# Sixteen rows apart instead of side by side: another assignment of DRAM blocks to SBUF partitions in a top-2 dispatch kernel

## The chip, the cores and the metric

The kernel runs on one core of a Trainium2 chip. The metric is device time in microseconds (us): 239.35 us is the median of three runs of the kernel before (239.24 to 239.37). One further execution was taken with the hardware profiler; all durations of single instructions and transfers come from that one.

## The reference

Each of 16 x 1024 tokens has a row of 512 floats (`x`) and 8 router logits. The softmax over the logits is taken, the two largest probabilities are kept and divided by their sum, and the row is written twice, once multiplied by the smaller and once by the larger of the two:

```
probs = softmax(router_logits)                     # over 8 experts
topk_indices = np.argsort(probs, axis=-1)[..., -k:]    # k = 2
topk_probs = np.take_along_axis(probs, topk_indices, axis=-1)
topk_probs = topk_probs / np.sum(topk_probs, axis=-1, keepdims=True)
return x[:, :, None, :].repeat(k, axis=2) * topk_probs[..., None]
```

So 33.55 MB of `x` and 0.52 MB of logits are read, and 67.11 MB are written. The arithmetic is one multiplication for each float written.

## The kernel before

**Tiling.** The 16384 tokens are 128 partitions times M = 128 rows. They are cut into two groups, `GROUPS = [69, 59]`: group 0 is the first 128 x 69 tokens, group 1 the other 128 x 59. Within a group each partition has one block of consecutive tokens (69 or 59 rows of 2 KB). The views `x_v`, `o_v` and `rl_v` (lines 93 to 95) say which block: partition p has block p. For a load of n rows each partition gets one run of n x 2 KB from DRAM; a store of n rows takes one run of n x 4 KB from each partition. Neighbouring partitions lie 69 x 2 KB = 138 KB (118 KB in group 1) apart in `x` and twice that in the output.

**Loads.** `LOADS` lists them: 7, 32 and 30 rows in group 0, and 30 and 29 rows in group 1 (line 114). After the first load come the two loads of the logits (lines 107 and 108). All are issued from SyncE (SP). The tile `xs` has 69 rows a partition, so the loads of group 1 overwrite rows of group 0, and wait until these have been used and stored.

**Weights.** `top2_weights` (lines 43 to 70) finds the two largest logits by maxima and minima on VectorE (DVE) and makes both weights `WA` with two sigmoids on ScalarE (ACT).

**Products and stores.** `STORES` lists five stores in group 0 and four in group 1, each of 13 to 15 rows. For each, VectorE multiplies rows of `xs` by their two weights in one instruction (line 128); in some of the pieces ScalarE does the last 1 or 4 rows (line 136). The products go to a second tile `osp` or to rows of `xs` that are already used up, by turns, and are stored from there (line 139), again from SP. An instruction that writes `osp` waits until the store that read it before has landed.

**Order.** Nothing is planned: the order of the program is the order on each engine. SP issues loads and stores in that order, one queue for all, and a store's issue waits for its product. All 16 transfers go through this one queue, `q1` in the profile, and each is spread over the core's 16 DMA engines.

## Time and profile before

| | us |
|---|---|
| median of three runs | 239.35 |
| the profiled execution, its own time | 241.59 |
| its span, first to last instruction | 239.8 |
| VectorE busy | 127.9 |
| ScalarE busy | 18.2 |
| DMA queue, share of 16 engines' span | 97.9% |

The profiled execution took 2.24 us longer than the median run, and 1.79 us of it lie outside its span. The line `DMA` of the page gives the mean busy share of the 16 DMA engines in 40 slices of 6 us, the line `GB/s` what they moved; a transfer's piece (packet) is booked in the slice in which it begins, so that a share of a short stretch can be above 1 and neighbouring slices swing around their mean. "SPq" is the issuing of transfers by SyncE.

### The profile page before, as it was taken

How to read it: one execution, taken by the hardware profiler on the slowest of the kernel's cores; microseconds unless marked ns; L12 is line 12 of the kernel's file. 1: busy time of each engine (PE TensorE's matmuls, PEld its weight loads, DVE VectorE, ACT ScalarE, POOL GpSimd, SP SyncE). 2: the span in 40 equal slices, each digit the busy share in tenths (PEclk: the TensorE clock that was granted, in tenths of full speed). 3: DMA queues.
4: the chain of work that ended last, by engine and by line, in shares of the span. 5: the costliest groups of instructions: out<-in, count | busy, mean ns of one | idle time of the engine just before them, and what ended most of it. 6: DMA issues, size and time to landing. Idle time of an engine off the chain costs nothing.

```text
span 239.8 us, 132 instructions
## 1 busy us (share of the span) xinstructions
DVE 127.9 (53%) x20; ACT 18.2 (8%) x29; POOL 0.2 (0%) x4
## 2 busy tenths in 40 slices
DVE  0410299997499990780000000999993999950000
ACT  2000000000440000700000000200000800000000
POOL 0000000000000000000000000000000000000000
DMA  7998989979999989999999799797979979979993
GB/s 263 480 503 372 482 348 492 451 344 440 459 459 459 440 373 411 459 459 448 426 426 460 328 492 471 327 476 332 482 338 492 482 338 492 482 338 481 450 450 172
DMA packets 2304, 101.19 MB, mean 422 GB/s; under 512 B 256, under 2 KB 384, under 8 KB 512
## 3 DMA queue, kind: packets, MB, share of 16 engines
q1 hardware_dynamic: 2304, 101.19, 97.9%
HBM read 34.08 MB, written 67.11 MB: 422 GB/s over the span
## 4 chain that ended last, share of the span: by engine, by line
DMA 53%; DVE 35%; SPq 1%; issue 0%; DVEq 0%
DMA xs<-in_x_dram 26%; DVE osp L128 22%; DMA out_dram<-osp 17%; DVE xs L128 13%; DMA out_dram<-xs 10%; SPq L108 0%; SPq L107 0%; SPq L114 0%; DVEq L128 0%; SPq L139 0%
## 5 line engine op out<-in xcount | busy, mean ns | idle before, releaser
L128 DVE TENSOR_TENSOR osp<-xs,WA 128x14336 f32<-128x14336 f32 (+3 forms) x5 | 62.7, 12532 | 75.7 <-DMA xs<-in_x_dram 58.9
L128 DVE TENSOR_TENSOR xs<-xs,WA 128x14336 f32<-128x14336 f32 (+1 forms) x4 | 61.4, 15359 | 0.3
L136 ACT ACTIVATE osp<-xs,WA 128x512 f32<-128x512 f32 x26 | 16.4, 709 | 161.2 <-DMA out_dram<-osp 113.2
L55 DVE TENSOR_TENSOR osp<-osp 128x512 f32<-128x512 f32 x1 | 0.7, 691 | 9.1 <-DMA osp<-in_router_logits_dram 9.1
L69 ACT ACT_TABLE_LOAD x1 | 1.3, 1283 | 0.7 <-PEq L157 0.7
L69 ACT ACTIVATE WA<-osp 128x128 f32<-128x128 f32 x1 | 0.3, 316 | 11.0 <-DVE osp L68 11.0
L56 DVE TENSOR_TENSOR osp<-osp 128x512 f32<-128x512 f32 x1 | 0.7, 693 | 0.0
L65 DVE TENSOR_TENSOR osp<-osp 128x256 f32<-128x256 f32 (+1 forms) x2 | 0.7, 353 | 0.0
L63 DVE TENSOR_TENSOR osp<-osp 128x256 f32<-128x256 f32 (+1 forms) x2 | 0.7, 352 | 0.0
L64 DVE TENSOR_TENSOR osp<-osp 128x256 f32<-128x256 f32 (+1 forms) x2 | 0.7, 352 | 0.0
L62 DVE TENSOR_TENSOR osp<-osp 128x256 f32<-128x256 f32 (+1 forms) x2 | 0.7, 352 | 0.0
L68 DVE TENSOR_TENSOR osp<-osp 128x128 f32<-128x128 f32 x1 | 0.3, 291 | 0.0
L70 ACT ACTIVATE WA<-osp 128x128 f32<-128x128 f32 x1 | 0.3, 296 | 0.0
L157 POOL MEMSET const-bfloat16-1.0<- 128x1 bf16 x1 | 0.1, 101 | 0.0
L157 POOL MEMSET const-uint8-127<- 128x1 uint8 x1 | 0.1, 101 | 0.0
L157 POOL MEMSET const-float32-0.0<- 128x1 f32 x1 | 0.1, 98 | 0.2 <-issue 0.2
L157 POOL MEMSET const-float32-1.0<- 128x1 f32 x1 | 0.1, 98 | 0.0
## 6 DMA issues: line engine op xcount, KB each, us to landing
out_dram<-xs SPq DMA_DIRECT2D x3, 7168.0 KB, 24.6
xs<-in_x_dram SPq DMA_DIRECT2D x2, 7680.0 KB, 40.0
out_dram<-osp SPq DMA_DIRECT2D x2, 7680.0 KB, 22.3
out_dram<-osp SPq DMA_DIRECT2D x2, 7168.0 KB, 21.3
out_dram<-xs SPq DMA_DIRECT2D x1, 7680.0 KB, 22.3
xs<-in_x_dram SPq DMA_DIRECT2D x1, 7424.0 KB, 53.3
out_dram<-osp SPq DMA_DIRECT2D x1, 6656.0 KB, 23.2
xs<-in_x_dram SPq DMA_DIRECT2D x1, 1792.0 KB, 6.9
```

The lines of the kernel that those rows point to most:

```text
L55: nc.vector.tensor_tensor(hi, a, b, op=ALU.max)
L56: nc.vector.tensor_tensor(lo, a, b, op=ALU.min)
L62: nc.vector.tensor_tensor(tmp, lo[:, :, 0:n], lo[:, :, n : 2 * n], op=ALU.max)
L63: nc.vector.tensor_tensor(nlo, a, b, op=ALU.min)
L64: nc.vector.tensor_tensor(nlo, nlo, tmp, op=ALU.max)
L65: nc.vector.tensor_tensor(nhi, a, b, op=ALU.max)
L68: nc.vector.tensor_tensor(dlt, hi, lo, op=ALU.subtract)
L69: nc.scalar.activation(WA[:, :, 0], dlt[:, :, 0], ACTF.Sigmoid, scale=-1.0)
L70: nc.scalar.activation(WA[:, :, 1], dlt[:, :, 0], ACTF.Sigmoid, scale=1.0)
L128: nc.vector.tensor_tensor(og[:, :v], xs[:, s : s + v, :].unsqueeze(2).to_broadcast([P, v, 2, D]), w[:, :v].unsqueeze(3).to_broadcast([P, v ...
L136: nc.scalar.activation(og[:, i, c], xs[:, s + i, :], ACTF.Copy, scale=w[:, i, c : c + 1])
L157: nc = _bacc.Bacc("TRN2", target_bir_lowering=False, num_devices=1)
```

## The change

Only the three views are changed. They cut the first dimension of a group into 8 x 16 blocks, `(b a m)`, and name `a` before `b`. The partitions of the tiles, 128 in one dimension, are met in the order a, then b: partition 8a + b gets the block of rows 16b + a of its group, where before it got block 8a + b. Logits, `x` and output are changed alike, so each token's weights are still in the partition of its row. The sizes of the runs, the number of loads and stores, their order, every instruction of VectorE and ScalarE and the tiles are as before. The view of DRAM now has dimensions 16, 8 and the rows in place of 128 and the rows, and its first two steps are those of one block (16 of them) and of 16 blocks (8 of them).

```diff
-        x_v.append(xf[t0:t1].rearrange("(p m) d -> p m d", p=P))
-        o_v.append(of[t0:t1].rearrange("(p m) k d -> p m k d", p=P))
-        rl_v.append(rf[t0:t1].rearrange("(p m) e -> p m e", p=P))
+        x_v.append(xf[t0:t1].rearrange("(b a m) d -> a b m d", a=16, b=8))
+        o_v.append(of[t0:t1].rearrange("(b a m) k d -> a b m k d", a=16, b=8))
+        rl_v.append(rf[t0:t1].rearrange("(b a m) e -> a b m e", a=16, b=8))
...
-            nc.sync.dma_start(xs[:, s : s + n, :], x_v[g][:, r : r + n, :])
+            nc.sync.dma_start(xs[:, s : s + n, :], x_v[g][:, :, r : r + n, :])
...
-            {"SP": nc.sync, "ACT": nc.scalar}[queue].dma_start(o_v[g][:, r : r + n], og)
+            {"SP": nc.sync, "ACT": nc.scalar}[queue].dma_start(o_v[g][:, :, r : r + n], og)
```

## Prediction

> **What bounds the kernel now.** I read the page's shares and slices first, then the DMA part, then the chain of waits in order of time, and last short windows of the DMA engines.

> ```profile
> span 239.8 us, 132 instructions
> DVE 127.9 (53%) x20; ACT 18.2 (8%) x29; POOL 0.2 (0%) x4
> ...
> GB/s 263 480 503 372 482 348 492 451 344 440 459 459 459 440 373 411 459 459 448 426 426 460 328 492 471 327 476 332 482 338 492 482 338 492 482 338 481 450 450 172
> DMA packets 2304, 101.19 MB, mean 422 GB/s; under 512 B 256, under 2 KB 384, under 8 KB 512
> ...
> q1 hardware_dynamic: 2304, 101.19, 97.9%
> ```

> The 16 DMA engines carry a packet 97.9% of the span, 0.979 x 239.8 = 234.8 us on each; 5.0 us are left. VectorE works 53% and has slack. The packets number 2304: 16 transfers x 128 partitions is 2048, and the 256 under 512 B are 16 for each transfer. So each partition's run is one packet.

> ```profile
> out_dram<-xs SPq DMA_DIRECT2D x3, 7168.0 KB, 24.6
> out_dram<-osp SPq DMA_DIRECT2D x2, 7680.0 KB, 22.3
> xs<-in_x_dram SPq DMA_DIRECT2D x1, 1792.0 KB, 6.9
> ```

> A store of 7168 KB is 57344 B a partition, and each DMA engine takes 8 such packets.

> ```profile
> 46.00:63.00 17.00, 12.68 (x1) 0.00 (x0) 0.00 (x0) 1.00 1.00 435
> 130.00:148.00 18.00, 0.00 (x0) 0.00 (x0) 0.00 (x0) 1.00 1.01 435
> ```

> These windows (columns: stretch, length, busy time of DVE, ACT and POOL, clock, DMA share, GB/s) show a stretch of stores and one of loads. Both run at 435 GB/s with the engines full, 27.2 GB/s each: reading DRAM and writing it cost alike. At that rate 101.19 MB take 232.6 us. The kernel is bound by 16 streams that each already run at one common rate; the most that any better order could save is 239.8 - 232.6 = 7.2 us, part of which is the start and the last landing.

> ```profile
> 46.60:47.60 1.00, 1.00 (x1) 0.00 (x0) 0.00 (x0) 1.00 0.26 115
> 47.60:48.00 0.40, 0.40 (x1) 0.00 (x0) 0.00 (x0) 1.00 3.97 1720
> 48.00:48.20 0.20, 0.20 (x1) 0.00 (x0) 0.00 (x0) 1.00 1.32 573
> 48.20:48.40 0.20, 0.20 (x1) 0.00 (x0) 0.00 (x0) 1.00 0.00 0
> ```

> A packet is booked where it begins. 115 GB/s over 1 us are 2 packets of 57344 B, 1720 over 0.4 us are 12, 573 over 0.2 us are 2: all 16 engines begin a packet within 0.6 us at most. They march in step, with 57344 B / 27.2 GB/s = 2.11 us a packet.

> ```profile
> 89.48 24.60 DMA out_dram<-xs
> ...
> 114.09 36.16 DMA xs<-in_x_dram
> ...
> 150.38 15.10 DVE osp L128
> ...
> 165.50 0.02 SPq L139
> ```

> ```profile
> 162.00:162.80 0.80, 0.80 (x1) 0.00 (x0) 0.00 (x0) 1.00 2.23 965
> 162.80:164.90 2.10, 2.10 (x1) 0.00 (x0) 0.00 (x0) 1.00 0.20 85
> 164.90:166.30 1.40, 1.31 (x2) 0.00 (x0) 0.00 (x0) 1.00 0.10 42
> 166.30:166.60 0.30, 0.30 (x1) 0.00 (x0) 0.00 (x0) 1.00 7.21 3072
> 166.60:167.60 1.00, 1.00 (x1) 0.00 (x0) 0.00 (x0) 1.00 0.14 61
> ```

> At one place in the chain the queue runs dry. The second group's first load lands at 150.25 us, VectorE takes 15.10 us, and the store is issued at 165.5 us, when most engines have done the last load. Of its packets (59392 B, 2.18 us each) 13 begin from 162.0 to 162.8 and end by 165.0; the next to begin, 15 at once (3072 GB/s over 0.3 us, of 61440 B), are the store's at 166.3. The sixteenth engine begins its own over 0.3 us later (61 GB/s, one packet). I put this hole at 1.4 us, 164.9 to 166.3.

> **The change part by part.** *Work.* The bytes, the run lengths and the 16 issues stay, and the work of VectorE and ScalarE is untouched. The line rate gives the same 232.6 us if the 16 engines still work at 27.2 GB/s each.

> *Issue.* The DRAM side now has one dimension more.

> ```profile
> L114 SPq DMA_DIRECT2D xs<-in_x_dram x5: 339/531/1219, 0.7 to 114.5; - x5
> L139 SPq DMA_DIRECT2D out_dram<-osp x5: 332/332/348, 43.6 to 198.0; - x5
> ```

> An issue takes 0.33 to 0.34 us at its fastest (columns after the colon: min/median/max ns). The trace has no issue of this shape. From below it costs nothing more, or even less; from above I double it, 0.34 us each. It lies beside running transfers except at the first load and at the dry place, so the upper end is 2 x 0.34 = 0.7 us, and 16 x 0.34 = 5.4 us if every issue counted. I take 0, as the number of descriptors is unchanged. The work hiding it is the queue's stock: the store at 89.48 us landed 24.60 us after issue, some 17 us of which are its own bytes (7.34 MB / 435 GB/s), so 7 us of older work lay ahead of it. Nothing is queued on SP behind an issue but the next wait for a product.

> *DRAM addresses.* Before, neighbouring partitions were 138 KB apart in `x`; now one step of b is 16 blocks, 2208 KB. Reads and writes, at different strides (138 KB in `x`, 276 KB in the output), ran alike at 435 GB/s, so I take 0 for this; from both sides, a gain is at most the 7.2 us above, and a loss is bounded by the slowest long slice of the page, 327 GB/s, 1.33 times as long.

> *Which engine serves which partition.* This is the term that decides. Before, both sides of a transfer counted 128 in one dimension, so the 128 packets could be dealt to the 16 engines in any pattern. Now the DRAM side counts 16, then 8, and the SBUF side 128. Both can be cut alike for 16 engines only as 16 consecutive pieces: engine a has partitions 8a to 8a + 7, in this order. My hypothesis for this kernel: the ways into SBUF are sixteen, each good for the 27.2 GB/s that one stream has in the windows, and each serving certain groups of partitions; before, each engine kept to one way, and now two engines are on the same way at a time, while half the ways are idle. The trace before shows no such sharing. Bounds from its rows: at the one end the packets still take 2.11 us (no effect; below that they can't go, since all 16 are at their rate); at the other, two streams at one rate, 4.2 us a packet, twice the 234.8 us.

> [...]

> *How far in step.* Let the two engines of a pair be apart by a lead. A run on one way is 4 packets, 8.4 us. During the lead they aren't in each other's way, so time is (2 - lead/run) times the present. All begin within 0.6 us, which is at most 7% of a run; but the late engine of the windows from 162.8 to 167.6 us shows that one can get behind by some packet's part: it begins one load packet in the hole, after the other engines' last ones began by more than 2 us (24%). Equal sharing keeps a lead as it is. I take 5%: a factor of 1.95.

> The sum: 234.8 x 1.95 = 457.9, plus the 5.0, minus the 1.4 us hole (the 29 rows that cover it now take twice as long, against unchanged 15.10 us of VectorE): a span of 461.5. With the 1.79 us outside the span, 463.3 stands against the profiled execution's 241.59. The median of the runs is 2.24 us lower: 461. No new wait opens: VectorE's 127.9 us are far below, and stores land later but queue behind as many older bytes as now, so that the queue stays full.

> **The rivals.** *Pairs that drift apart.* If one engine of a pair gets more of the shared way, it pulls ahead until it is on the other way while its partner is on the first; from then on both run at full rate. For it: 0.6 us is no firm lock, and a lead of 2 us occurs. Against: nothing in the rows favours one engine steadily. A single full run's lead costs 8.4 us, 239.35 + 8.4 = 248; half way, a factor of 1.4 gives 239.35 + 0.4 x 234.8 = 333. So 250 to 414 for part, ending where it becomes my forecast (1.75).

> *Nothing happens.* If each engine's rate is its own limit and not SBUF's, or the pieces are dealt as before, the 2.11 us a packet stay and the time is 239.35. The windows speak for it in so far as an engine's rate and a way's rate can't be told apart there.

> *Slightly slower.* DRAM addresses or the longer issue take some per cent: 5.4 us of issues give 244.8. Against: all covers named above. 240 to 250.

> *Faster, by one mechanism.* The late engine holds back the first load of the second group, and with it the store at 165.5 us. If its lateness comes from its DRAM blocks, and the new blocks end it while the engines keep 27.2 GB/s, the load lands earlier and the hole of 1.4 us closes: 237.9. It decides as soon as that load lands 1.4 us before 150.25. Against: no other window shows an engine that late, so it looks like a single event.

> **How the numbers follow.** The forecast, pairs sharing, has 0.54; its own range goes from a factor of 1.75 (234.8 x 1.75 + 5.0 - 1.4 - 0.45 = 414; 0.45 is 2.24 - 1.79) to a factor of 2 with the hole kept and all issues dearer (469.6 + 5.0 - 0.45 + 5.4 = 480). Partial drift has 0.20, slightly slower 0.08, nothing 0.13, faster 0.05. A measurement of this kernel tells about 0.2%, 0.5 us, from no change. Slower is 0.54 + 0.20 + 0.08 = 0.82, same 0.13, faster 0.05. Leaving out same and faster (0.18) and a little of the rest, the range is 243 to 480.

> **What would show it.** Right: the slices' GB/s fall to about 220 over the whole span, the DMA share stays above 95% (each engine still holds a packet all the time), a 7168 KB store lands some 45 us after its issue in place of 24.6, the hole before the first store of group 1 is gone, and VectorE's 127.9 us stay. Packets stay at 2304; more of them would mean that runs were cut. A share near 50% at the same 220 GB/s would mean that only 8 engines are used: the time of the forecast by another cause. Full rate with one pair-like lag between early and late engines would show drift. Unchanged 435 GB/s in the windows would show the hypothesis wrong at its root: engines, not ways into SBUF, set the rate.

## The result and the profile after

The changed kernel takes 443.51 us (median of four runs, 437.46 to 444.64) against 239.36. The ratio is 1.839, with a 95% interval of 1.820 to 1.859; it is taken from the two faster of the four runs (437.46 and 442.92), as the other two count as slow, and the medians as they stand give 1.853. Its profiled execution is the fastest of the four, 437.46 us with a span of 435.7.

The page of the changed kernel, the lines that answer to those shown of before:

```profile
span 435.7 us, 132 instructions
## 1 busy us (share of the span) xinstructions
DVE 127.9 (29%) x20; ACT 18.2 (4%) x29; POOL 0.2 (0%) x4
...
GB/s 179 243 253 217 187 181 254 197 300 205 247 211 253 247 200 253 279 258 205 282 274 266 214 231 217 218 218 249 332 265 299 271 197 237 259 244 238 253 137 21
DMA packets 2304, 101.19 MB, mean 232 GB/s; under 512 B 256, under 2 KB 384, under 8 KB 512
## 3 DMA queue, kind: packets, MB, share of 16 engines
q1 hardware_dynamic: 2304, 101.19, 95.6%
```

The same bytes move in the same 2304 packets, VectorE is as busy as before, and the DMA engines still hold a packet 95.6% of the span. They only move 232 GB/s instead of 422. Each packet takes longer; nothing else is added. The last two slices (137 and 21 GB/s) are new: the engines no longer finish together.

Windows of the changed kernel: one stretch of the first group's loads, the first group's stores, the second group's loads, the second group's stores.

```profile
54.00:86.00 32.00, 30.12 (x2) 0.00 (x0) 0.00 (x0) 1.00 1.02 211
90.00:242.00 152.00, 35.68 (x3) 10.02 (x16) 0.00 (x0) 1.00 1.01 251
244.00:312.00 68.00, 31.25 (x2) 1.33 (x2) 0.00 (x0) 1.00 0.99 233
316.00:433.00 117.00, 26.98 (x2) 5.01 (x8) 0.00 (x0) 1.00 0.87 226
```

The first group's loads run at 211 GB/s where 435 stood before, a factor of 2.06. Stores are a little better: 251 GB/s over the first group (the last 12 us of that window hold loads of the second group too), and 226 over the second, where the share of 0.87 says that some engines were already without work. The second group's loads, which follow the stores, run at 233.

The DMA issues and the issuing lines of the changed kernel:

```profile
out_dram<-xs SPq DMA_DIRECT2D x3, 7168.0 KB, 69.0
out_dram<-osp SPq DMA_DIRECT2D x2, 7680.0 KB, 50.1
...
xs<-in_x_dram SPq DMA_DIRECT2D x1, 1792.0 KB, 10.9
```

```profile
L115 SPq DMA_DIRECT2D xs<-in_x_dram x5: 586/598/2552, 0.7 to 215.9; - x5
L140 SPq DMA_DIRECT2D out_dram<-osp x5: 537/538/591, 69.1 to 356.2; - x5
```

The stores of these rows land 50 to 69 us after their issue in place of 22 to 25, and an issue takes 0.54 to 0.59 us at its fastest in place of 0.33 to 0.34. The latter is real, but 16 times 0.25 us beside running transfers explains nothing of 200 us.

### The profile page after: what moved, and what is told of

Read it like the earlier page. It is cut to its first block, busy times and chain, and to the rows that moved or that the text cites. A ratio compares the mean times of both kernels' runs of the same rounds, so it can differ in the third digit from the quotient of the medians.

```text
span 435.7 us, 132 instructions
## 1 busy us (share of the span) xinstructions
DVE 127.9 (29%) x20; ACT 18.2 (4%) x29; POOL 0.2 (0%) x4
## 2 busy tenths in 40 slices
DMA packets 2304, 101.19 MB, mean 232 GB/s; under 512 B 256, under 2 KB 384, under 8 KB 512
## 3 DMA queue, kind: packets, MB, share of 16 engines
q1 hardware_dynamic: 2304, 101.19, 95.6%
## 4 chain that ended last, share of the span: by engine, by line
another core or an unknown queue 34%; DVE 26%; DMA 25%; SPq 0%; issue 0%; DVEq 0%
DMA out_dram<-osp 22%; DVE osp L129 14%; DVE xs L129 10%; DMA osp<-in_router_logits_dram 3%; DVE osp L55 0%; DVE osp L56 0%; SPq L115 0%; SPq L108 0%; DVE osp L64 0%; DVE osp L65 0%; DVE osp L63 0%; DVE osp L62 0%; DVE osp L68 0%; DVEq L129 0%
## 5 line engine op out<-in xcount | busy, mean ns | idle before, releaser
L69 ACT ACTIVATE WA<-osp 128x128 f32<-128x128 f32 x1 | 0.3, 315 | 15.6 <-DVE osp L68 15.6
## 6 DMA issues: line engine op xcount, KB each, us to landing
out_dram<-xs SPq DMA_DIRECT2D x3, 7168.0 KB, 69.0
xs<-in_x_dram SPq DMA_DIRECT2D x2, 7680.0 KB, 76.4
out_dram<-osp SPq DMA_DIRECT2D x2, 7680.0 KB, 50.1
out_dram<-osp SPq DMA_DIRECT2D x2, 7168.0 KB, 52.4
out_dram<-xs SPq DMA_DIRECT2D x1, 7680.0 KB, 65.0
xs<-in_x_dram SPq DMA_DIRECT2D x1, 1792.0 KB, 10.9
```

Source lines behind the costliest of these rows:

```text
L69: nc.scalar.activation(WA[:, :, 0], dlt[:, :, 0], ACTF.Sigmoid, scale=-1.0)
```

## The experiments

### The same mixing, cut 32 x 4 and 64 x 2

```diff
-        x_v.append(xf[t0:t1].rearrange("(b a m) d -> a b m d", a=16, b=8))
+        x_v.append(xf[t0:t1].rearrange("(b a m) d -> a b m d", a=32, b=4))
...
```

`o_v` and `rl_v` are changed alike; the second kernel has a=64, b=2.

> The views keep the mixing of the blocks but cut 32 x 4 in place of 16 x 8: partition 4a + b gets block 32b + a. The DRAM side counts 32, then 4, so each engine can be given two groups of four neighbouring partitions that need not be side by side. Theory of the ways into SBUF (the cut decides which partitions an engine has at a time): each engine can keep to one way, packets of 57344 B take 2.11 us, 239.4 us within 1%. Rival, DRAM addresses (neighbouring blocks read and written by all engines at once, and large steps within a partition group): as with 16 x 8, about 440 us. Rival, a third dimension on the DRAM side makes transfers slow by itself: about 440 us too. [...]

> The views cut 64 x 2: partition 2a + b gets block 64b + a. As with 32 x 4 each engine can be given groups of four neighbouring partitions. Theory of the ways: 239.4 to 242 us. The 32 x 4 cut took 0.9% over the kernel before. If that is the price of a third dimension in each issue (0.67 us in place of 0.38 for the first), it is the same here, 241.6; if it is the order of the blocks in DRAM, it may differ, 239.4 to 241.6. Rival, mixing of blocks as such: about 440.

Measured: 241.65 us for 32 x 4 (1.0089 of before, 1.0068 to 1.0110) and 241.64 us for 64 x 2 (1.0071, 1.0040 to 1.0102). Windows of the 32 x 4 kernel, a stretch of stores and one of loads, and its issuing of loads:

```profile
47.00:63.00 16.00, 12.02 (x1) 0.00 (x0) 0.00 (x0) 1.00 0.99 430
134.00:148.00 14.00, 0.00 (x0) 0.00 (x0) 0.00 (x0) 1.00 1.00 430
```

```profile
L115 SPq DMA_DIRECT2D xs<-in_x_dram x5: 591/612/1389, 0.7 to 115.1; - x5
```

The blocks are mixed here too, neighbouring blocks are in use at once, and the DRAM view has three dimensions with the dearer issue. All of that together costs 2.2 to 2.3 us. Both rivals fall. What the 16 x 8 cut does beyond it costs 202 us. Where the 2.3 us come from isn't settled: the two mixings cost the same, which fits the issue, but the first issue explains only 0.3 us (0.67 us with 32 x 4 against 0.38 before), and single runs of the kernel before take 241.3 us too; its profiled execution took 241.59.

### The cut alone, blocks side by side

```diff
-GROUPS = [69, 59]
+GROUPS = [69, 58]
...
-        t1 = t0 + P * n
-        x_v.append(xf[t0:t1].rearrange("(b a m) d -> a b m d", a=16, b=8))
...
+        t1 = t0 + 16 * (8 * n + 4)
+        xg = xf[t0:t1].rearrange("(a r) d -> a r d", a=16)[:, : 8 * n]
...
+        x_v.append(xg.rearrange("a (b m) d -> a b m d", b=8))
```

`o_v` and `rl_v` are cut alike, and the last load and the last store have a row less. This kernel leaves out 128 of the 16384 tokens.

> The blocks stay side by side as before (partition 8a + b has block 8a + b), but after each eighth partition four rows are skipped, so that the DRAM side can't be written as one dimension of 128 and counts 16, then 8, as in the changed kernel. To make room the second group has 58 rows in place of 59: 128 of 16384 tokens are left out, 0.8% of the bytes. Theory of the ways: the cut into 16 consecutive pieces is all that matters, so 1.84 x 0.992 x 239.4 = about 437 us (420 to 450), and the first long load lands at 54 us in place of 28. Rival, DRAM addresses: the order of the blocks is as before, so 237.5 us.

Measured: 430.76 us (two runs, 427.47 and 434.05). With 0.8% fewer bytes this is the changed kernel's time within 3%, though partition 8a + b has block 8a + b as before. The cut into 16 and 8 is enough; the mixing isn't needed.

### Loads alone, stores alone

The loads-alone kernel is the changed one with the store views of before; the stores-alone kernel is the one before with the store views of the changed one. The first of the two, against the changed kernel:

```diff
-        o_v.append(of[t0:t1].rearrange("(b a m) k d -> a b m k d", a=16, b=8))
+        o_v.append(of[t0:t1].rearrange("(p m) k d -> p m k d", p=P))
...
```

> Only the loads of x and logits take the changed views, the stores have the old ones; the rows of the output land at other tokens' places. Theory of the ways: the loads' 34.1 MB (78 us at 435 GB/s) take 2.1 times as long as in the changed kernel's first 50 us, the stores go at 435 GB/s again: 239.4 + 1.1 x 78 = 325 us, less if the loads' engines drift apart. Rival, only the writing of DRAM suffers: 239.4 us.

> Only the stores take the changed view, the loads have the old ones; the rows of the output land at other tokens' places. Theory of the ways: the stores' 67.1 MB (154 us at 435 GB/s) take up to 2.1 times as long, less as the two engines of a pair drift apart: about 443.5 - 325 + 239.4 = 358 us (330 to 400). Rival, only the reading of DRAM or the filling of SBUF suffers: 239.4 us.

Measured: 323.61 us with the loads changed, 381.09 with the stores changed. First the windows of the loads-alone kernel (loads, then stores), then those of the stores-alone kernel (loads, then the stores of each group):

```profile
12.00:86.00 74.00, 34.01 (x13) 0.51 (x2) 0.00 (x0) 1.00 1.01 211
92.00:160.00 68.00, 35.68 (x3) 10.02 (x16) 0.00 (x0) 1.00 0.99 431
```

```profile
8.00:44.00 36.00, 19.52 (x13) 0.51 (x2) 0.00 (x0) 1.00 1.03 447
50.00:190.00 140.00, 44.17 (x4) 10.02 (x16) 0.00 (x0) 1.00 1.00 246
230.00:370.00 140.00, 48.01 (x4) 5.01 (x8) 0.00 (x0) 1.00 0.96 221
```

There is one run of each, and both kernels put rows of the output at other tokens' places. Each side pays for itself, and the other runs at the old rate. The loads cost 84.3 us over 239.3, the stores 141.8. The sum, 226, is more than the 204 of both together. The durations of the packets in the traces, summed and divided by the 16 engines, show where it is given back: the stores' packets take 282.3 us with the stores alone changed and 259.5 in the changed kernel, the loads' 163.2 with the loads alone changed and 156.9 in the changed kernel. Engines that are further apart when the second group comes would explain it; that is argued, not shown.

### The place of the partitions alone

To measure the ways by themselves, ten loads of one shape were put ahead of the kernel before, each overlapping the last so that it waits for it:

```diff
+    def probe(p0, p1, n, s=39):
+        nc.sync.dma_start(
+            xs[p0:p1, s : s + n, :],
+            xf[: n * (p1 - p0)].rearrange("(p m) d -> p m d", p=p1 - p0),
+        )
...
+    probe(32, 96, 30)
+    probe(0, 64, 30)
...
```

> The kernel before with ten loads of x ahead of it, one after the other (each overlaps the one before and waits for its landing), 61440 B a partition into later rows of xs: partitions 0-127, 0-63, 32-95, 64-127, 0-127, 32-95, 0-63, 0-127, 16-47, 32-47. Nothing is left out; only time is added. Theory of the ways into SBUF, with sixteen ways of which partitions 0-63 have eight and 64-127 the other eight, and four neighbouring partitions to a way: 128 partitions 18 us of transfer, 0-63 and 64-127 at half the rate also 18 us, 32-95 at the full rate 9 us, 16-47 on eight ways 9 us, 32-47 on four ways 9 us, all with 1 to 2 us of latency. Rival, the engines alone set the rate: 64 partitions 9 us wherever they lie, 32 partitions 4.5 us, 16 partitions 2.3 us. [...]

The program's scheduler put the body's first stages between the first four (of these, the load to 64 to 127 ran at 205 GB/s from 104.0 to 118.4 us), so the last six are read, which followed one another with nothing beside them. Windows inside them: partitions 0-127, 32-95, 0-63, 0-127, 16-47, 32-47; the last two windows hold the whole transfer with its start.

```profile
139.00:152.60 13.60, 0.00 (x0) 0.00 (x0) 0.00 (x0) 1.00 1.00 434
160.00:166.80 6.80, 0.00 (x0) 0.00 (x0) 0.00 (x0) 1.00 1.00 434
173.50:187.90 14.40, 0.00 (x0) 0.00 (x0) 0.00 (x0) 1.00 1.00 205
194.00:207.60 13.60, 0.00 (x0) 0.00 (x0) 0.00 (x0) 1.00 1.00 434
212.00:224.00 12.00, 0.00 (x0) 0.00 (x0) 0.00 (x0) 1.00 0.77 164
224.50:234.50 10.00, 0.00 (x0) 0.00 (x0) 0.00 (x0) 1.00 0.79 98
```

Two loads of 64 partitions with the same bytes from the same rows of DRAM run at 434 GB/s when they go to partitions 32 to 95, and at 205 when they go to 0 to 63. In the first four windows every engine holds a packet (share 1.00); between these two loads only the place differs. Divided by their shares, the last two windows give 164 / 0.77 = 213 and 98 / 0.79 = 124 GB/s, half and something over a quarter. Place decides, in about the steps that the expectation set down for shared ways. The 124 is more than the four ways it gave to 32 to 47 would carry at 27.1 GB/s each (434 / 16), 108 in all, so a fixed rate for each way doesn't describe four engines on one. Where by the theory two engines are on one way, in 0 to 63, they lose more than half: 434 / 205 = 2.12.

### A lead between the engines of a pair

If two engines meet on a way, letting one of each pair begin a run of four packets later should free both without touching the views. In the kernel with a lead of half a run each loop has `range(2)`.

```diff
+    for i in range(4):
+        delay(12, i)          # one packet on each of engines 0 to 11
+    for i in range(4):
+        delay(8, 48 + i)      # on engines 0 to 7
+    for i in range(4):
+        delay(4, 80 + i)      # on engines 0 to 3
```

> The changed kernel, with twelve more loads ahead of the first: four for engines 0 to 11, four for 0 to 7, four for 0 to 3, each of one 61440 B packet an engine (into rows of xs that a later load overwrites). Engines 0 to 3 then start 12 packets late, 4 to 7 eight, 8 to 11 four, 12 to 15 none: the two engines of each supposed pair (e and e + 4) begin one run of four packets apart. Views, addresses and cut are those of the changed kernel. Theory of the ways: each engine is on one way while its partner is on the other, most packets take the 2.1 to 2.4 us of the kernel before, and the time is 239.4 plus the 12 packets of the latest engines (27 us, or up to twice that if these loads get in each other's way): 267 to 300 us. Rival, DRAM addresses or the cut's shape as such: 443.5 + 27 = 470 us.

> As the run with a lead of one run, with two loads of each kind in place of four: a lead of half a run. Theory of the ways with equal sharing: half of each run is shared, a factor of 1.5 on 234.8 us, 239.4 + 117 + 14 = 370 us (330 to 400, since leads can grow). Rival, addresses or shape: 443.5 + 14 = 457 us.

Measured: 484.73 us and 451.54 us. Both expectations failed. Windows of the kernel with a lead of one run, the delaying loads and a stretch of the long loads, and below them a stretch of the long loads with half a run:

```profile
6.00:20.00 14.00, 0.00 (x0) 0.00 (x0) 0.00 (x0) 1.00 0.73 154
75.00:115.00 40.00, 3.82 (x11) 0.51 (x2) 0.00 (x0) 1.00 0.97 201
```

```profile
54.00:86.00 32.00, 3.55 (x1) 0.00 (x0) 0.00 (x0) 1.00 0.97 229
```

The twelve delaying loads held SP's queue (four times SP waited for an earlier one to land, 13.8 us in all), and the kernel's own first load was issued only at 24.45 us. By the count of the packets, engines 12 to 15 were idle until then (the share of 0.73 is that of twelve engines), and got no lead over 8 to 11. But engines 0 to 3 should still have trailed 4 to 7, and yet all sixteen ran at 201 GB/s. With half a run the first load went out at 5.17 us, and the long loads ran at 229 GB/s, little better than the 211 of the changed kernel; why half a run brought so little is open. So either the theory was wrong, or one pair on a shared way holds up every load. The next run was made to tell these apart: pure loads ahead of the body, small packets, and two delays behind which the queue stays full.

```diff
+    for i in range(7):
+        cut16(i)              # 8 rows of x with the 16 x 8 view, 16384 B a partition
+    delay(12, 0)              # four packets on each of engines 0 to 11
+    delay(4, 48)              # four more on engines 0 to 3
+    for i in range(7):
+        cut16(i)
+    for i in range(4):
+        sixteen(16 + i, 0)    # every fourth partition from 16 + i, one an engine
+    for i in range(4):
+        sixteen(32 + i, 16)
```

> Before the body of the kernel before, four rows of loads of x into rows that are loaded again later; nothing is left out, only time is added. (1) Seven loads with the changed kernel's 16 x 8 view, 16384 B a partition. (2) Two loads that hold engines 0 to 11 by four such packets and engines 0 to 3 by another four, then the seven loads again: now the engines of the supposed pairs (e and e + 4) are one run of four packets apart. (3) Four loads of 16 partitions, one an engine, every fourth partition from 16 to 79 and their neighbours, 32768 B: by the map of ways engines 0 to 3 share with 8 to 11, the others are alone. (4) The same from 32 to 95: all are alone. A packet of 16384 B takes 0.60 us at the full rate, one of 32768 B 1.21. Theory of the ways: (1) 2.1 times that, 1.28 us; (2) 0.60 us for nearly all once the delays are through; (4) 1.21 us. The run with delays before the changed kernel failed to free the loads; if that was because engines 8 to 15 stayed together there and a shared way slows all loads, also those that are alone, then (3) is 2.55 us for all sixteen; if each is slowed alone, (3) has half its packets at 1.21 and half at 2.55. Rival (a load cut into 16 consecutive pieces is slow whatever the others do): (2) 1.28 us.

Windows: the first seven loads (two rows), the same seven after the delays, the loads of 16 partitions, and the end of these.

```profile
8.00:40.00 32.00, 0.00 (x0) 0.00 (x0) 0.00 (x0) 1.00 1.01 217
40.00:72.00 32.00, 0.00 (x0) 0.00 (x0) 0.00 (x0) 1.00 1.01 216
84.00:106.00 22.00, 0.00 (x0) 0.00 (x0) 0.00 (x0) 1.00 1.01 416
116.90:129.40 12.50, 0.00 (x0) 0.00 (x0) 0.00 (x0) 1.00 1.02 207
131.40:132.60 1.20, 0.00 (x0) 0.00 (x0) 0.00 (x0) 1.00 1.05 376
```

The same seven loads, with the same view, addresses and cut, run at 216 GB/s when the engines begin together and at 416 when engines e and e + 4 are a run apart. That shows that engines a run apart free each other, and that neither the view nor the addresses are slow in themselves. The same delays also put e and e + 8 a run apart. That the partners are e and e + 4 follows only together with the loads to partitions 0 to 63, which share among themselves (205 GB/s). The first seven hold their 217 and 216 GB/s for 64 us: among loads a pair that meets stays together.

The third row of loads ran at 207 GB/s as a whole. Eight engines at the full 27.1 GB/s (434 / 16) beside eight at 12.8 (205 / 16) would give about 320. So the unshared ones went as slowly as the shared. The fourth row overlapped with it on engines that were ahead, and reached its full pace only when the third was over. (The 376 GB/s of the last window hold twelve of its packets and four of the body's first load.) The trace's durations of single packets say the same: all packets of these two rows that began from 112 to 129 us took 2.4 to 2.9 us, and all twenty that began after 131 us took 1.21 or 1.22.

That some engines shared nothing needs little of the theory. By their order, the twelve packets that began at 131.5 to 131.8 us went to every fourth partition from 32 to 76 or to neighbours of these; they ran at the full pace side by side, so these places have a way each. The third row has these twelve and four more (16 to 28), which can meet at most four of them; at least eight packets at a time had no partner, and none was fast. The 154 GB/s of twelve engines above (12.8 each, of which four have no partner by the theory) agree: every packet that began in that window's first 8 us took 4.7 to 4.8 us. When only the eight engines of the next delaying loads were left, at 23 us, a packet took 2.27. So a shared way slows all loads, also those that share nothing, in both kernels in which it was looked for. Why is open.

### The same for stores

> The test of the lead, for stores: before the body, 32 rows of x are loaded (in the old order of blocks) and stored by seven stores with the 16 x 8 view, 16384 B a partition, into rows of the output that the body writes again later; then one such store on engines 0 to 11 and one on 0 to 3, each of four packets an engine, put these behind, and seven more stores follow. Nothing is left out, only time is added. Theory of the ways: reading SBUF is shared as writing it is, so the first seven run at about half rate, 210 to 260 GB/s (1.0 to 1.28 us a packet of 16384 B, with some engines getting ahead as in the changed kernel's stores), and the second seven, one run apart, at 400 GB/s or more (0.60 us a packet). Rival (stores are slow for another reason, such as writing DRAM in this order): both at the same 210 to 260 GB/s. If a lead is lost among stores, the second seven begin fast and slow down.

Windows of this kernel: the first seven stores (four rows), then those after the delays (three rows).

```profile
42.00:44.00 2.00, 0.00 (x0) 0.00 (x0) 0.00 (x0) 1.00 1.00 426
46.00:48.00 2.00, 0.00 (x0) 0.00 (x0) 0.00 (x0) 1.00 1.01 270
59.00:67.00 8.00, 0.00 (x0) 0.00 (x0) 0.00 (x0) 1.00 0.97 391
67.00:79.00 12.00, 0.00 (x0) 0.00 (x0) 0.00 (x0) 1.00 1.01 429
97.00:105.00 8.00, 0.00 (x0) 0.00 (x0) 0.00 (x0) 1.00 0.96 248
105.00:113.00 8.00, 0.00 (x0) 0.00 (x0) 0.00 (x0) 1.00 0.99 334
121.00:129.00 8.00, 0.00 (x0) 0.00 (x0) 0.00 (x0) 1.00 0.97 403
```

The run did not test what it was built for. The second delaying store writes rows that the first writes too, waited for it, and was issued only at 94.33 us; one of the second seven stores had gone ahead at 49.34, the queue ran almost empty at about 93 us, and the last six began with only engines 0 to 3 put back.

The expectation missed in an instructive way: stores need no delays. After 270 GB/s at 46 us they reach 429 within about 25 us, and from the second start 248 becomes 403 in about as long. The engines come apart by themselves. The view that writes DRAM in this order reaches 429 GB/s, so it isn't slow either. Unlike among loads, fast packets (0.61 us) and slow ones (1.2 us) run side by side here.

One observation doesn't fit the picture of ways. The first stores begin at 426 GB/s, although all engines begin within 0.7 us, and slow down only after some four packets each. The changed kernel does the same when its first stores follow the loads:

```profile
89.40:93.80 4.40, 0.00 (x0) 0.00 (x0) 0.00 (x0) 1.00 1.00 417
```

The kernel with the stores alone changed does not: of its first sixteen store packets twelve took 3.4 us or more. Why they run free in the other two is open. For stores, then, it is shown that the cut costs (stores alone, 381.09 us) and that the same view runs freely once the engines are apart; that it is the ways of SBUF on which they meet, as with loads, is argued.

A run here is 4 x 16384 B, 2.4 us at the full rate; in the kernel a run is three to four times as long, so the same coming apart should take longer. Whether it is undone when engines wait for one another is not shown.

## Why the prediction was right

The forecast was 461 us against 443.5 measured. The mechanism it named, two engines at a time on half of the ways, is borne out for the loads and argued for the stores. Point by point:

- **What bounds the kernel.** Right. Work of VectorE and ScalarE, bytes and packets are unchanged, and the time follows the packets. Of the signs that were named, one missed: a 7168 KB store landed 69.0 us after its issue, not some 45.
- **DRAM addresses taken at 0.** Nearly right: 32 x 4 and 64 x 2 mix the blocks at a price of 2.2 to 2.3 us, part of which may be something else; the cut alone without mixing gives 430.76 us.
- **Issue taken at 0.** Right for the sum. Its price per issue was inside the bounds (0.59 against 0.34 us, where the upper end was the double).
- **Which engine serves which partition.** Right, for loads. The place of partitions alone halves the rate (434 to 205 GB/s), and a lead between e and e + 4 takes the halving away (216 to 416 GB/s). The deal itself is inferred from these effects, as the trace doesn't say which engine a packet ran on, and no run counts the ways. Of the two ends that stood there, the engines' 234.8 us unchanged and twice as long, the result (416.5 us) is nearer to the second.
- **The factor of 1.95.** Mis-sized, by more than any other term. The engines' busy time is 0.956 x 435.7 = 416.5 us in place of 457.9, a factor of 1.77. By the durations of the packets, summed and divided by 16, the loads took 156.9 us in place of 79.4 (1.98) and the stores 259.5 in place of 155.3 (1.67). So the factor was near for the loads and too high for the stores. The run of 4 packets, on which the 5% rests, was the author's assumption and stands in no row of before; loads four packets apart, freed from 216 to 416 GB/s, agree with it. The other step behind the factor, "equal sharing keeps a lead as it is", holds for loads and not for stores: stores pull apart, so that the rival of pairs that drift was half true. That the engines of a pair slow only each other is too narrow for loads (207 GB/s with eight of sixteen unshared), which changed nothing here, where all engines are in pairs. Nor was the double the upper end: loads in step cost 2.12 times (434 / 205).
- **The rest of the span.** The sum had 5.0 - 1.4 = 3.6 us; it is 435.7 - 416.5 = 19.2. Engines that have come apart don't end together (137 and 21 GB/s in the last slices): after 410 us they are idle for 13.6 us in the mean. Another 3.1 us lie between 340 and 360, where engines that were ahead had no stores left until the one issued at 356.24 us. So "the queue stays full" was wrong too. Neither step was in the sum.
- **From profile to median.** I subtracted 2.24 us as for the kernel before; here the profiled execution was 6.05 us below the median. The four runs spread over 7.2 us, while all runs of the kernel before on record lie between 239.22 and 241.59. That the engines come apart differently from run to run would explain it, but only one execution was profiled.
- **The total.** The busy time came 41.4 us under the forecast, the rest of the span 15.6 over it, and the step from the span to the median 8.3 over it. More than half of the large miss was thus made up by two others: that the total came as near as it did is in part luck.

## What to carry to other kernels

The order of dimensions in a DRAM view can decide not only addresses but, by all that these runs show, which engine gets which SBUF partitions. Here a view whose outermost count is 16 cost a factor of 1.84, as if each engine had been handed eight neighbouring partitions, while 32 x 4 and 64 x 2 with the same mixing stayed within 1%. A DMA share near 100% doesn't mean the full rate (95.6% stood beside 232 GB/s here, 97.9% beside 422): divide bytes by time and compare with what the same engines reach elsewhere in the trace. Where a rate is halved at full share, look for engines in step on a shared way, and test it by putting them out of step (216 to 416 GB/s for loads here).

## What was not expected of the hardware

- Two engines on one way lose more than half: 434 to 205 GB/s (2.12 times) for loads to partitions 0 to 63, and about the same for the changed view (435 to 211, 2.06 times).
- Loads that share ways don't drift (217, then 216 GB/s over 64 us) and slow loads that share nothing (no packet begun from 112 to 129 us under 2.4 us, where 1.21 is the full pace). Stores come apart by themselves, from 248 to 403 GB/s in 30 us, and first run at 426 GB/s for two microseconds. Why reading and writing SBUF differ in this is open.
- 64 partitions, well placed (32 to 95), take the full 434 GB/s.
